# The order of the two products in the wide weight blocks of a two-layer decoder trunk

## The chip, the cores and the metric

The kernel runs on one core of one Trainium2 chip. The metric is the device time of one execution in microseconds (us). The time before is the median of three runs. The profile is one further execution with the hardware profiler on.

## What is computed

A trunk of two pre-norm residual layers on 256 tokens of width 1024, in float32. Layer 0 mixes tokens with a short gated convolution, layer 1 with dilated window attention in three groups of eight heads. After the mixer each layer has a squared-ReLU MLP (1024 to 4096 to 1024) and a gated input embedding.

```python
for i in range(2):
    hn = rmsnorm(h, norm_mix[i])
    mixed = short_conv_mixer(hn, ...) if i == 0 else dilated_attention_mixer(hn, positions, w_qkv, w_o)
    h = h + mixed
    h = h + squared_relu_mlp(rmsnorm(h, norm_mlp[i]), mlp_w_up[i], mlp_w_down[i])
    ple_gate = sigmoid(rmsnorm(h, norm_ple[i]) @ ple_w_gate[i])
    h = h + ple_gate * (p[i] @ ple_w_proj[i])
return rmsnorm(h, norm_final)
```

Nearly all of the work is in dense products of activations with weights: `w_in`, `w_out`, `w_qkv`, `w_o`, `w_up`, `w_down` and the gates.

## The kernel before, in words

**High and low parts.** TensorE multiplies in a reduced float32 format here (`F32R`). To keep the accuracy, every weight and activation is split into a high part (rounded to that format) and a low part (the rest). A product is then three products: low weight by high activation, high weight by low activation, high weight by high activation.

**Weights.** All weights are packed on the host in the order in which they are used, into slabs of up to eight 128x128 tiles (`make_slabs`, L230). `load_to` (L324) loads slabs from HBM. `split_to` (L333) makes the high part `whi` with a ScalarE copy (L340) and the low part `wlo` with a VectorE subtraction (`sub`, L288 and L289). So `wlo` is always later than `whi` of the same slab.

**Blocks.** `make_plan` (L134) writes out the whole order of the work as a list. Each entry is a block (one 128x128 weight tile times the activations) or a step ("do"). The list fixes the order of TensorE's instructions; the other engines' steps are placed among them by a scheduler, and the steps in `URGENT` get a higher priority. `block` (L351) emits the matmuls of one entry, all through the one call at L374. There are three kinds:

- kind "n" (L358): three products of 256 columns, into one half of a PSUM bank.
- kind "w" (L361), the wide blocks: two products. The low weights times the high activations have 256 columns and go to the first half of the bank. The high weights times both parts of the activations have 512 columns and fill the whole bank. `sums` (L389) later adds the halves. Each output column tile of 128 has a bank of its own; tiles come in pairs, `half` 0 and 1, which take turns on every 128 rows `k` of the contraction.
- kind "t" (L367): three products with the weights as the moving operand.

The wide blocks are used for the third input of the convolution (`sc_in`, tile `acc_X`), for the queries and keys of heads 1 to 7 (`qkv`, `acc_qk`), and for both MLPs (`up`, `acc_u`, and `down`, `acc_d`).

**Order within a wide block.** At L364 the tuple `products` lists the low product first and the high one second. L366 turns the tuple round for `half` 1, except for `qkv`. With `half` 0 and 1 alternating, TensorE's order over a pair of blocks is: low, high, high, low. For `qkv` it is: low, high, low, high. The first matmul into a bank has `start` set, whichever it is.

**Around it.** `h_ready` (L417) makes the high part of the next activations on ScalarE (L422) and the low part on VectorE (L423). `mix_out` (L577) and `up_out` (L581) call it or do the same, and `head_start` (L51) orders the first blocks of an MLP, so that the activations made last are used last. The gate of layer 0 (`gate_out`, L599) and the first `qkv` blocks follow the MLP of layer 0.

Of the kernel before, what the change touches and what calls it, by code (L numbers as in the profile page):

```python
# [213 lines left out]
def width(key):  # L214
    return {"v": GROUPS, "gate1": 4, "proj1": 4}.get(key, 1)
# [32 lines left out]
def tile_trunk(ctx: ExitStack, tc: tile.TileContext, plan, slabs, ap, out):  # L248
# [25 lines left out]
    def bank(name):  # L274
        return psum.tile([P, 2, S], F32, tag="ps", name=name)
# [9 lines left out]
    def flat(t):  # L285
        return t.rearrange("p i s -> p (i s)")
# [16 lines left out]
    for op in plan:  # L303
        if op[0] != "do":
            key = ((*op[4], op[5]), 0) if op[0] == "w" else (op[4], op[5] if op[0] == "n" else 0)
# [38 lines left out]
    def weights(item):  # L344
        si, at = place[item]
        split_to(si + min(LOOK, 1 + si // 3))
        hi, lo = parts[si]
        n = width(item[0]) * P
        return hi[:, at : at + n], lo[:, at : at + n]

    def block(kind, key, k, col, name, half, operand, m=0, cuts=1):  # L351
        name = (*name, half) if kind == "w" else name
        if name not in opened:
            acc[name] = bank("acc_" + "_".join(map(str, name)))
        left[name, half if kind == "n" else 0] -= 1
        whi, wlo = weights((key, k, col))
        x = state[operand][k // 2]
        if kind == "n":  # L358
            dst = acc[name][:, half, :]
            products = ((dst, wlo, x[0][:, k % 2, :]), (dst, whi, x[1][:, k % 2, :]), (dst, whi, x[0][:, k % 2, :]))  # L360
        elif kind == "w":  # L361

            dst = acc[name]
            products = ((dst[:, 0, :], wlo, x[0][:, k % 2, :]), (flat(dst), whi, flat(x[2][:, k % 2, :, :])))  # L364

            products = products[::-1] if half and key != "qkv" else products  # L366
        else:  # L367
            n = width(key) * P // cuts
            whi, wlo = (t[:, m * n : (m + 1) * n] for t in (whi, wlo))
            dst = flat(acc[name])[:, :n]  # L370
            xhi, xlo = (t[:, k % 2, half * P : (half + 1) * P] for t in x[:2])
            products = ((dst, xhi, whi), (dst, xhi, wlo), (dst, xlo, whi))
        for n, (to, a, b) in enumerate(products):
            nc.tensor.matmul(  # L374
                to,
                a,
                b,
                start=n == 0 and name not in opened,
                stop=n == len(products) - 1 and left[name, half if kind == "n" else 0] == 0,
                skip_group_check=True,  # L380
            )
            opened.add(name)
# [414 lines left out]
    for op in plan:  # L797
        if op[0] != "do":
            block(*op)
        elif op[1] in URGENT:  # L800
            with tc.high_priority(offset=HURRY):
                steps[op[1]](*op[2:])
        else:
            steps[op[1]](*op[2:])
# [87 lines left out]
```

## Time and profile before

| what | value |
|---|---|
| time, median of 3 runs | 785.04 us (784.73 to 785.06) |
| the profiled execution's own time | 785.37 us |
| its span, first to last instruction | 783.5 us |
| PE (TensorE matmul) busy | 772.6 us, 99% of the span |
| PEld (TensorE weight load) busy | 703.1 us, 90% |
| DVE (VectorE) busy | 575.8 us, 73% |
| ACT (ScalarE) busy | 439.7 us, 56% |
| POOL (GpSimd) busy | 167.6 us, 21% |
| HBM traffic over the span | 179 GB/s |

The profiled execution is 0.33 us over the median of the runs, and 1.9 us of its time lie outside the span. Matmuls are pipelined: the profile draws a matmul's end later than the start of the next, so durations of matmuls overlap, and the time that one costs is read from start to start or from the chain of work that ended last, which counts each stretch once.

### The profile page before, as it was taken

To read this page: it belongs to the slowest core of one execution; us is meant where nothing else is said; L and a number is where in the kernel's file an instruction comes from. 1 tells how busy PE (TensorE), PEld (TensorE's weight loads), DVE (VectorE), ACT (ScalarE), POOL (GpSimd) and SP (SyncE) were. 2 spreads that over 40 slices of the span, in tenths; PEclk is the share of its full clock that TensorE was granted. 3 is DMA by queue.
4 is the path that set the end of the run, shared out by engine and by line. 5 is a ranking of instruction groups with operands and counts; after the bars stand their busy time and mean duration, and the time that the engine had idled before them with its cause. 6 is when DMAs were issued, how large, how long until landed. Compare 5 with 4: busy or idle time off the path is not lost.

```text
span 783.5 us, 12521 instructions
## 1 busy us (share of the span) xinstructions
PE 772.6 (99%) x4858; PEld 703.1 (90%) x4858; DVE 575.8 (73%) x831; ACT 439.7 (56%) x674; POOL 167.6 (21%) x109
## 2 busy tenths in 40 slices
PE   9999999999999999999999999999999999999995
PEld 9999998888888899989989989989988888888884
DVE  6997779898566668888768768767598887655654
ACT  7654565565444446557655655655575555444452
POOL 0000000000000000177867867865000000000001
PEclk9999999999999999999999999999999999999998
DMA  8966555656565554555555455556456565565521
GB/s 288 313 199 191 177 189 177 197 177 202 189 194 187 191 180 147 184 191 156 156 173 163 149 174 163 152 170 194 157 165 187 190 190 191 187 190 194 188 80 54
DMA packets 41819, 140.97 MB, mean 180 GB/s; under 512 B 4768, under 2 KB 5152, under 8 KB 41760
## 3 DMA queue, kind: packets, MB, share of 16 engines
q1 hardware_dynamic: 41328, 139.61, 55.8%
q8 instruction: 38, 0.62, 0.3%
q10 hardware_dynamic: 432, 0.56, 0.2%
q14 instruction: 21, 0.17, 0.1%
HBM read 139.10 MB, written 1.05 MB: 179 GB/s over the span
## 4 chain that ended last, share of the span: by engine, by line
PE 95%; DVE 2%; issue 1%; DMA 1%; ACT 0%; POOL 0%; SPq 0%; POOLq 0%; ACTq 0%
PE acc_u L374 23%; PE acc_d L374 23%; PE acc_qk L374 15%; PE acc_v L374 9%; PE acc_o L374 6%; PE acc_g L374 5%; PE acc_C L374 3%; PE acc_B L374 3%; PE acc_X L374 3%; PE acc_p L374 1%; PE o L693 1%; PE sc L654 1%; PE tp L672 1%; DVE wlo L289 1%; PE sc L651 1%
## 5 line engine op out<-in xcount | busy, mean ns | idle before, releaser
L289 DVE TENSOR_TENSOR wlo<-raw,whi 128x1024 fp32r<-128x1024 f32 (+3 forms) x274 | 350.6, 1285 | 161.9 <-ACT whi L340 159.6
L340 ACT ACTIVATE whi<-raw 128x1024 fp32r<-128x1024 f32 (+3 forms) x274 | 278.0, 1016 | 225.7 <-PE acc_d L374 77.1
L374 PE MATMUL acc_u<-x,whi 128*128 128x512 f32 x512 | 160.9, 396 | 0.0
L374 PE MATMUL acc_d<-u,whi 128*128 128x512 f32 x512 | 160.8, 395 | 0.0
L374 PE MATMUL acc_qk<-x,whi 128*128 128x512 f32 (+1 forms) x432 | 134.8, 369 | 0.8 <-DVE x L423 0.8
L446 POOL TENSOR_TENSOR n<-v,power 128x4 f32<-128x4 f32 (+1 forms) x6 | 5.6, 937 | 521.5 <-DVE v L466 519.4
L374 PEld LDWEIGHTS acc_d<-u,wlo 128*128 128x128 f32 x512 | 96.2, 188 | 22.7
L374 PEld LDWEIGHTS acc_u<-x,wlo 128*128 128x128 f32 x512 | 96.2, 188 | 22.6
L374 PE MATMUL acc_qk<-x,wlo 128*128 128x256 f32 x384 | 107.5, 281 | 0.0
L374 PE MATMUL acc_u<-x,wlo 128*128 128x256 f32 x512 | 101.2, 278 | 0.0
L374 PE MATMUL acc_d<-u,wlo 128*128 128x256 f32 x512 | 100.9, 278 | 0.0
L374 PEld LDWEIGHTS acc_qk<-x,whi 128*128 128x128 f32 x432 | 77.7, 188 | 14.8 <-DVE x L423 1.2
L621 POOL TENSOR_TENSOR rot<-qk,sinr 16x512 f32<-16x512 f32 x44 | 78.3, 1781 | 3.0
L374 PEld LDWEIGHTS acc_u<-x,whi 128*128 128x128 f32 x512 | 77.9, 189 | 0.1
L374 PEld LDWEIGHTS acc_d<-u,whi 128*128 128x128 f32 x512 | 78.0, 189 | 0.0
L374 PEld LDWEIGHTS acc_qk<-x,wlo 128*128 128x128 f32 x384 | 72.3, 189 | 0.2 <-ACT x L422 0.2
L374 PE MATMUL acc_v<-whi,x 128*128 128x384 f32 x256 | 68.8, 339 | 0.0
L618 POOL TENSOR_TENSOR qk<-qk,cosr 128x512 f32<-128x512 f32 x22 | 36.7, 1669 | 52.4 <-DVE qk L394 41.9
L374 PEld LDWEIGHTS acc_v<-whi,x 128*128 128x128 f32 x256 | 46.6, 188 | 0.0
L374 PE MATMUL acc_o<-y,whi 128*128 128x256 f32 x256 | 46.0, 283 | 0.0
L627 POOL TENSOR_TENSOR qk<-qk,rot 48x512 f32<-48x512 f32 x22 | 42.9, 1949 | 1.7
L374 PE MATMUL acc_v<-wlo,x 128*128 128x384 f32 x128 | 42.8, 335 | 0.0
(169 smaller groups left out, 1040.0 us busy)
## 6 DMA issues: line engine op xcount, KB each, us to landing
raw<-in_w SPq DMA_DIRECT2D x231, 512.0 KB, 3.6
raw<-in_w SPq DMA_DIRECT2D x32, 384.0 KB, 3.1
raw<-in_w SPq DMA_DIRECT2D x9, 256.0 KB, 5.2
h<-in_xT SPq DMA_DIRECT2D x4, 256.0 KB, 5.9
out<-ht SPq DMA_DIRECT2D x3, 256.0 KB, 2.0
mask<-in_mask SPq DMA_DIRECT2D x2, 256.0 KB, 4.3
gain<-in_gain SPq DMA_DIRECT2D x2, 256.0 KB, 4.3
pt<-in_pT ACTq DMA_DIRECT2D x1, 256.0 KB, 3.2
```

Of the source, the lines that this page charges most:

```text
L289: nc.vector.tensor_tensor(out, a, f32(b), ALU.subtract)
L340: nc.scalar.activation(hi[:, :width], t[:, :width], AF.Copy)
L374: nc.tensor.matmul(to, a, b, start=n == 0 and name not in opened, stop=n == len(products) - 1 and left[name, half if kind == "n" else 0] == 0,
L446: nc.gpsimd.tensor_tensor(y, v, power[:, : v.shape[1]], ALU.pow)
L618: engine.tensor_tensor(t, p, both(cosr), ALU.mult)
L621: engine.tensor_tensor(r[dst : dst + 16], p[src : src + 16], sinr[src : src + 16].unsqueeze(1).to_broadcast([16, 2, S]), ALU.mult,)
L627: engine.tensor_tensor(t[:48], t[:48], r[:48], ALU.add)
L651: nc.tensor.matmul(ps[:, :S], q[:, 0, own], k[:, 1, :], start=n == 0, stop=n == 2)
L654: nc.tensor.matmul(ps[:, (g + 1) * P : (g + 2) * P], t[:, 0, own], t[:, 1, own], start=True, stop=True)
L672: nc.tensor.transpose(ps[n // 2][:, n % 2, b * P : (b + 1) * P], sm[:, n * P : (n + 1) * P], ident)
L693: nc.tensor.matmul(ps[:, 0, b * P : (b + 1) * P], v12[:, b, g * P : (g + 1) * P], t[:, g, b * P : (b + 1) * P], start=False, stop=g == 1, ...
```

## The change

One line of `block` is changed. The tuple is now turned round for every wide block except those of `qkv`, so the 512-column product with the high weights comes first and the 256-column product with the low weights second, in both halves. `qkv` keeps low first. Over a pair of blocks TensorE's order becomes: high, low, high, low. The blocks, their operands, their banks and the number of instructions stay the same.

```diff
@@ -363,7 +363,7 @@
             dst = acc[name]
             products = ((dst[:, 0, :], wlo, x[0][:, k % 2, :]), (flat(dst), whi, flat(x[2][:, k % 2, :, :])))
 
-            products = products[::-1] if half and key != "qkv" else products
+            products = products if key == "qkv" else products[::-1]
```

## Rows read from the trace of the kernel before

**Rows 1.** The page, busy time by engine, and the chain's shares by engine.

```profile
PE 772.6 (99%) x4858; PEld 703.1 (90%) x4858; DVE 575.8 (73%) x831; ACT 439.7 (56%) x674; POOL 167.6 (21%) x109
...
PE 95%; DVE 2%; issue 1%; DMA 1%; ACT 0%; POOL 0%; SPq 0%; POOLq 0%; ACTq 0%
```

**Rows 2.** The chain in order of time: start, length, work, instructions; pieces of layer 0.

```profile
15.23 1.40 PE acc_X L374 x8
...
35.65 2.10 PE acc_X L374 x12
...
38.30 3.50 PE acc_X L374 x20
...
53.31 5.58 PE acc_X L374 x32
58.88 5.76 PE acc_B L374 x48
...
104.77 22.30 PE acc_u L374 x128
127.30 66.89 PE acc_u L374 x384
194.20 89.17 PE acc_d L374 x512
```

**Rows 3.** The chain again, pieces of layer 1.

```profile
335.22 16.65 PE acc_qk L374 x96
...
400.54 11.11 PE acc_qk L374 x64
...
566.79 22.50 PE acc_u L374 x128
```

**Rows 4.** PE's timeline inside a run of query and key blocks: start, drawn length.

```profile
401.77 0.28 PE L374 MATMUL acc_qk<-x,wlo 128*128 128x256 f32 x1
401.89 0.39 PE L374 MATMUL acc_qk<-x,whi 128*128 128x512 f32 x1
...
411.25 0.40 PE L374 MATMUL acc_qk<-x,whi 128*128 128x512 f32 x1
```

**Rows 5.** PE's timeline at the end, projection products of 512 columns, kind "t".

```profile
766.79 0.39 PE L374 MATMUL acc_p<-whi,p 128*128 128x512 f32 x1
767.02 0.39 PE L374 MATMUL acc_p<-wlo,p 128*128 128x512 f32 x1
767.24 0.62 PE L374 MATMUL acc_p<-whi,p 128*128 128x512 f32 x2
...
768.15 0.39 PE L374 MATMUL acc_g<-whi,x 128*128 128x512 f32 x1
```

**Rows 6.** Stretches: length, busy (instructions) of each engine, PEclk, DMA share, GB/s.

```profile
194.20:283.30 89.10, 89.10 (x513) 77.73 (x513) 51.59 (x60) 40.91 (x51) 0.00 (x0) 1.00 0.58 189
...
335.20:351.80 16.60, 16.60 (x98) 14.51 (x97) 15.03 (x19) 8.42 (x15) 10.94 (x6) 1.00 0.61 189
```

**Rows 7.** Timelines of PE, then DVE, at the head of the MLP of layer 1.

```profile
566.62 0.28 PE L374 MATMUL acc_u<-x,wlo 128*128 128x256 f32 x1
566.84 0.73 PE L374 MATMUL acc_u<-x,whi 128*128 128x512 f32 x2
567.41 0.40 PE L374 MATMUL acc_u<-x,wlo 128*128 128x256 f32 x2
...
566.30 0.89 DVE L423 SCALAR_TENSOR_TENSOR x<-hr,gains,x 128x256 fp32r<-128x256 f32 x2
```

**Rows 8.** The chain once more, between the gate of layer 0 and the attention.

```profile
305.63 0.60 DVE gs L601
306.23 1.13 DVE wlo L289
...
320.68 0.87 DVE wlo L289
322.00 1.46 PE acc_qk L374 x10
```

## The prediction

> **What bounds the kernel now.** I read the page first [rows 1]: TensorE's matmuls are busy 99% of the span, and the chain of work that ended last runs over TensorE for 95% of it. VectorE and ScalarE have a quarter and more of their time free. So a nanosecond saved on TensorE in such a stretch is a nanosecond of the whole, and I need the price of a block, to a tenth of a percent.
>
> That price can't come from the drawn durations, since matmuls overlap (a 512-column matmul is drawn 0.39 us long, and the next starts after 0.23 [rows 4]). It comes from the chain in order of time, where each stretch counts once: length divided by blocks, two instructions to a wide block. The reader is to see two prices for the same two matmuls. Where pairs run low, high, high, low, the down projection takes 89.17 us for 512 instructions, 348.32 ns a block, and the up projection 66.89 us for 384, 348.39 ns [rows 2]. Where every block runs low, high (queries and keys), a run of 96 takes 16.65 us, 346.88 ns a block [rows 3].
>
> The third view is TensorE's own timeline inside such a run, away from its ends. From the high product at 401.89 to the one at 411.25 there are 27 blocks (the rows between repeat the pattern): 9.36 us, 346.67 ns a block [rows 4]. So the steady price of strict alternation is 346.67 ns, and a run's ends add a few hundredths of a microsecond.
>
> Last, the stretches: the granted clock is 1.00 (of 2.4 GHz) in both the down projection and a run of queries and keys, and weight loads are busy 87% of the time in each (77.73 of 89.10 us and 14.51 of 16.60 [rows 6]). Neither clock nor weight traffic sets the two stretches apart.
>
> **Why I put the difference down to the order.** Streams of one size show what each matmul costs without any mixing. The 256-column products of the convolution take 5.76 us for 48, 120.0 ns each [rows 2]. The 512-column products at the end take 766.79 to 768.15, 1.36 us for six, 226.7 ns each [rows 5]. Together 346.7 ns: exactly the alternating price. Alternation therefore costs nothing over its parts, and low, high, high, low costs about 1.65 ns a block more. Two high products in a row and two low ones in a row are what only the dearer pattern has.
>
> **The change part by part.** *What it touches.* Of each pair, only half 0 is turned round; half 1 is high first already. Wide blocks outside `qkv`: 512 of up and 512 of down (two layers of 128 plus 384 plus 512 instructions, over two), and 64 of the convolution's third input. 1088 blocks lie in 544 pairs; nothing is added or removed, no DMA, no instruction of another engine.
>
> *MLPs.* By the chain, layer 0 spends 22.30 + 66.89 + 89.17 = 178.36 us on 512 blocks [rows 2]. At 346.67 ns they take 177.49: 0.87 less. I take 0.85, leaving 0.02 for the ends of the runs (the 96-instruction run costs 16.65 against 48 × 0.34667 = 16.64). Layer 1 repeats it with 22.50 for its first piece [rows 3], whose extra 0.20 is a stall that I treat below. Both layers: -1.70 us. The bounds: by the dearest run of queries and keys, 11.11 us for 32 blocks or 347.19 ns [rows 3], the gain is 178.36 - 177.76 = 0.60 a layer, -1.20 in all; by the steady price and no ends, -1.74. I choose near the second, since these runs are 64 to 256 blocks long and the ends weigh little.
>
> *Convolution input.* Its 64 blocks take four pieces of 1.40 (the first is shown), one of 2.10, one of 3.50 and two of 5.58 (one shown), 22.36 us [rows 2]; at the steady price 22.19, -0.17. The pieces are of four to sixteen blocks, so ends weigh more here: I take -0.10, bounds 0 and -0.17.
>
> *The first block of an MLP.* High first needs the low part of the activations, which low first does not. In layer 0 the pieces before and after meet without a gap. In layer 1 TensorE starts the low product at 566.62 and the high one at 566.84, 0.10 us later than the 0.12 that such a step takes, since VectorE makes the low activations from 566.30, two of them in 0.89 us, the first ready near 566.75 [rows 7]. After the change the high product comes first and still can't start before 566.84; the low product then falls behind it instead of into the wait. Price +0.12 us (one low step); bounds 0 (the next high product, 0.34 us behind, absorbs it) and +0.22 (the whole wait).
>
> *The first use of a slab.* High first asks for `whi` a step earlier and for `wlo` a step later. `whi` is the older of the two, and TensorE has no idle time inside the up and down runs, so I cost it at nothing. The cover is the slabs split ahead; were it gone, the wait would move to the low product and be shorter by the high product's 0.23 us. Half 1 still ends with its low product, so slabs and banks come free in the same order as now.
>
> *Where the saved time goes.* After the MLP of layer 0, the chain passes to VectorE for the gate (305.63 to 322.00), with weight splits of 0.87 to 1.13 us in it [rows 8]. That chain starts from the gate's last products, so it moves forward with them; I cost it at nothing. If the order of VectorE's work changes there, a split more or less in the chain is ±1 us; that is a rival.
>
> *Sum.* -1.70 - 0.10 + 0.12 = -1.68 us. The profiled execution, 785.37, would become 783.69. It stands 0.33 above the median of the runs, so the runs would show 785.04 - 1.68 = 783.36 us, 0.21% less. A measurement of this kernel can tell about 0.2%, 1.57 us, from no change: the forecast lies just beyond that edge, and the chances are split accordingly.
>
> **A rule against it.** The same 768 columns in two matmuls cost 346.67 ns in one order and 348.3 in the other [rows 2, 4]. The Trainium skill, TensorE: Matmul & The Clock Gate, section Back-to-back issue gap, gives the gap of a warm matmul by its column count alone, N / 2.4 + 2.5 ns. By that a block takes 325 ns in any order, and the change brings 0 us. The trace speaks against the figure (both prices are over 20 ns higher) and, less surely, against the independence of order.
>
> **The rivals.** *Order does nothing.* The 1.65 ns could belong to something else that sets up and down apart from queries and keys, such as which tiles are read. For it: no row shows up or down in alternating order. Against: the convolution's input, which reads other tiles, shows 5.58 / 16 = 348.75 with the paired order [rows 2], and the sum of the parts fits alternation. Time: 785.04 us, or 785.16 with the late first block.
>
> *Low after high into the same bank is what costs.* This one ends slower. Queries and keys run low then high into a bank, then go to the other bank; they never write low onto the columns that high has just written. Up and down do it once a pair. If that one step held the whole excess, 2 × 1.65 = 3.3 ns, the change would double it: 350.0 ns a block, +1.65 × 1088 = +1.8 us, 786.8 us. It decides wherever an up block comes out above 348.4 ns. Against it: the 512-column products of the end go high, low, high into one bank at 226.7 ns each, with no excess [rows 5]; but there all three cover the same columns.
>
> *The gate's chain is reshuffled.* A scheduler places VectorE's instructions among each other, and a changed TensorE order may move a weight split into or out of the 16 us in which VectorE sets the pace [rows 8]. One split is 0.87 to 1.13 us, say 1.0: 782.4 us if one leaves, 784.4 if one enters. For it: splits stand in that chain more than once. Against: both orders take the same operands and almost the same time, so the scheduler has little to react to.
>
> **How the numbers follow.** The forecast, alternation at about 346.7 ns, has 0.67; within it the edge at 783.47 is 0.11 us away, and the bounds reach from 783.1 (-1.74 - 0.17 + 0) to 784.1 (-1.20 - 0 + 0.22), so I give it 0.44 faster and 0.23 same. Order does nothing: 0.13, same. Low after high: 0.07, slower (its 786.8 lies just beyond the edge at 786.61). A split leaves: 0.07, faster; one enters: 0.06, same. Faster 0.51, same 0.42, slower 0.07. The likeliest gives 783.36 us. The range from 782.5 to 784.9 holds the forecast and its bounds, nearly all of the late split and the fast half of the split that leaves: 0.67 + 0.06 + 0.04, and with a little of the case without effect about 0.8.
>
> **What would show it.** In the profile after, the chain's piece of the down projection should be 88.75 us instead of 89.17, and the long piece of up 66.56 instead of 66.89, on TensorE's timeline with single rows high, low, high, low and no x2. The piece of the convolution should fall from 5.58 to about 5.55, the queries and keys should stay. The first piece of up in layer 1 should be 22.4, with the wait on the low activations ahead of a high product. Any of these stretches above its old length would put the bank rival ahead; unchanged lengths, the first one. If the stretches shrink as said and the time does not, the saved time went into the chain from 305 to 322 us, which would then be longer than 16.4 us by what is missing.

## The result, and the profile after

The changed kernel takes 787.58 us (median of 8 runs, 786.9 to 790.55) against 785.28 us of the kernel before (8 runs, 784.73 to 785.78). The ratio is 1.0038, with a 95% interval of 1.0026 to 1.0049: slower by 0.38%, where 0.21% faster was forecast. The profiled execution took 787.52 us, 2.15 us more than that of before.

The chain of waits in order of time (start, length, work, instructions), changed kernel; the pieces that answer to [rows 2, 3] and [rows 8]:

```profile
15.02 1.41 PE acc_X L374 x8
...
35.49 2.13 PE acc_X L374 x12
...
38.08 3.47 PE acc_X L374 x20
...
53.05 5.65 PE acc_X L374 x32
...
104.67 22.62 PE acc_u L374 x128
...
127.52 67.84 PE acc_u L374 x384
195.36 90.45 PE acc_d L374 x512
...
324.39 1.45 PE acc_qk L374 x10
...
337.61 16.65 PE acc_qk L374 x96
...
569.31 22.85 PE acc_u L374 x128
...
592.40 66.56 PE acc_u L374 x384
658.97 88.75 PE acc_d L374 x512
```

The reader is to see one program at two prices. In layer 1 the long piece of up and the piece of down have exactly the forecast lengths, 66.56 and 88.75 us, 346.67 ns a block. In layer 0 the same two pieces, with the same order and the same shapes, take 67.84 and 90.45 us: 353.3 ns a block, dearer than the 348.3 of before [rows 2]. The convolution shows both within one pair of columns: 2.13 us for 6 blocks is 355, 3.47 for 10 is 347. Queries and keys, which the change leaves alone, are unchanged at 16.65.

The balance closes. Layer 0: 180.91 against 178.36, +2.55. Layer 1: 178.16 against 178.56, -0.40. The convolution (four pieces of 1.41, then 2.13, 3.47, 5.65 and one of 5.64): 22.53 against 22.36, +0.17. Together +2.32; the start-up before the first convolution block was 0.21 us shorter. The sum is 2.11 of the 2.15 us.

Stretches of the changed kernel, TensorE alone (length, busy with instructions, granted clock, DMA share, GB/s), layer 0 and layer 1:

```profile
127.52:195.30 67.78, 67.78 (x386) 1.00 0.59 187
592.40:658.90 66.50, 66.50 (x386) 1.00 0.62 190
```

The granted clock is 1.00 in both, so the clock is not the difference. TensorE's own timeline, first in layer 0, then in layer 1, shows what is:

```profile
139.73 0.40 PE L374 MATMUL acc_u<-x,whi 128*128 128x512 f32 x1
139.97 0.28 PE L374 MATMUL acc_u<-x,wlo 128*128 128x256 f32 x1
140.08 0.40 PE L374 MATMUL acc_u<-x,whi 128*128 128x512 f32 x1
140.31 0.28 PE L374 MATMUL acc_u<-x,wlo 128*128 128x256 f32 x1
140.43 0.40 PE L374 MATMUL acc_u<-x,whi 128*128 128x512 f32 x1
140.67 0.28 PE L374 MATMUL acc_u<-x,wlo 128*128 128x256 f32 x1
140.79 0.40 PE L374 MATMUL acc_u<-x,whi 128*128 128x512 f32 x1
...
619.63 0.39 PE L374 MATMUL acc_u<-x,whi 128*128 128x512 f32 x1
619.86 0.28 PE L374 MATMUL acc_u<-x,wlo 128*128 128x256 f32 x1
...
620.67 0.39 PE L374 MATMUL acc_u<-x,whi 128*128 128x512 f32 x1
```

No wait stands in either. Three blocks take 1.06 us from 139.73 to 140.79, and 1.04 from 619.63 to 620.67; in the first the steps go round in a pattern that repeats every three blocks (high products of 0.24, 0.23 and 0.24). In the nanoseconds of the trace its blocks take 350, 350 and 360, again and again, those of layer 1 346 or 347. So strict alternation has two steady patterns, 346.7 and 353.3 ns a block, and here it stays in the one it is in: down of each layer goes on in the pattern that up left. Below they are called the cheap and the dear pattern.

### The profile page after: what moved, and what is told of

It reads as the page before. It is cut to its first block, busy times and chain, and to the rows that moved or that the text cites. A ratio compares the mean times of both kernels' runs of the same rounds, so it can differ in the third digit from the quotient of the medians.

```text
span 785.7 us, 12525 instructions
## 1 busy us (share of the span) xinstructions
PE 774.0 (99%) x4858; PEld 704.7 (90%) x4858; DVE 575.6 (73%) x831; ACT 439.5 (56%) x674; POOL 167.6 (21%) x109
## 4 chain that ended last, share of the span: by engine, by line
PE 95%; DVE 2%; issue 1%; DMA 1%; ACT 0%; POOL 0%; POOLq 0%; SPq 0%; ACTq 0%
PE acc_u L374 23%; PE acc_d L374 23%; PE acc_qk L374 15%; PE acc_v L374 8%; PE acc_o L374 6%; PE acc_g L374 5%; PE acc_C L374 3%; PE acc_B L374 3%; PE acc_X L374 3%; PE acc_p L374 1%; PE o L693 1%; PE sc L654 1%; PE tp L672 1%; DVE wlo L289 1%; PE sc L651 1%
## 5 line engine op out<-in xcount | busy, mean ns | idle before, releaser
L374 PE MATMUL acc_u<-x,whi 128*128 128x512 f32 x512 | 179.9, 396 | 0.1
L374 PE MATMUL acc_d<-u,whi 128*128 128x512 f32 x512 | 179.3, 395 | 0.0
L374 PE MATMUL acc_u<-x,wlo 128*128 128x256 f32 x512 | 143.6, 281 | 0.0
L374 PE MATMUL acc_d<-u,wlo 128*128 128x256 f32 x512 | 143.6, 280 | 0.0
L374 PEld LDWEIGHTS acc_u<-x,whi 128*128 128x128 f32 x512 | 96.0, 188 | 23.1 <-PE acc_o L374 0.3
L374 PEld LDWEIGHTS acc_d<-u,whi 128*128 128x128 f32 x512 | 96.0, 187 | 22.5
```

Of the source, the lines that this page charges most:

```text
L374: nc.tensor.matmul(to, a, b, start=n == 0 and name not in opened, stop=n == len(products) - 1 and left[name, half if kind == "n" else 0] == 0,
```

## The experiments: what decides between the two patterns

Each kernel below is the changed kernel with the edit shown; times of before are from the same chip and series.

### Low first everywhere

```diff
-            products = products if key == "qkv" else products[::-1]
```

> Every wide block runs low first, as queries and keys do. Bank theory (a low product onto columns that the high product has just written lets TensorE settle into 353.3 ns a block; a low product into another bank does not): no such step is left, so all up, down and convolution runs at 346.7 ns, down 88.75 us in both layers, time 783.5 us. Entry theory (any strict alternation can run at 346.7 or 353.3 ns, and the first product of the run decides, high first being the risky one): the same 783.5. Chance theory (every break before a run draws one of the two patterns anew, whatever the order): some runs at 353.3, time between 784 and 790 us, differing between executions by 0.5 to 3.4 us.

790.06 us (789.94 to 790.24, 4 runs), ratio to before 1.0068 [1.0053, 1.0083]. Chain, this kernel:

```profile
127.55 67.84 PE acc_u L373 x384
195.40 90.45 PE acc_d L373 x512
...
337.67 16.65 PE acc_qk L373 x96
...
592.16 67.84 PE acc_u L373 x384
660.01 90.45 PE acc_d L373 x512
```

This was the test that I had thought safe in either theory, and it failed both. Up and down now run exactly as queries and keys do, low then high, and take the dear pattern in both layers, while queries and keys keep the cheap one. Neither the bank nor which product comes first can be the reason.

### The low product into another bank, and a low start with the banks as changed

Both kernels hold back the second product of half 0 until half 1 is out, which gives high 0, low 1, high 1, low 0, and low 0, high 1, low 1, high 0. The edit of the first is shown, without its changes to `start` and `stop`; the second has `and half` in place of `and not half`.

```diff
-            products = products if key == "qkv" else products[::-1]
+            products = products[::-1] if key != "qkv" and not half else products
...
+        if kind == "w" and key != "qkv":
+            if half:
+                todo.append(held_back.pop())
+            else:
+                held_back.append(todo.pop())
```

> Order over a pair: high 0, low 1, high 1, low 0. TensorE sees high, low, high, low and a run starts with high, as after the change, but every low product goes to another bank than the high one before it. Bank theory: no run at 353.3 ns, 783.5 us. Entry theory: the first runs of both layers at 353.3 ns as after the change, about 787.5 us. Chance theory: a mixture, 784 to 790 us.

> Order over a pair: low 0, high 1, low 1, high 0. A run starts with low, and every low product but the first goes onto columns that the high product has just written, as after the change. Bank theory: runs at 353.3 ns, 786 to 790 us. Entry theory: all runs at 346.7 ns, 783.5 us. Chance theory: a mixture, 784 to 790 us.

The first took 787.77 us (787.19 to 790.34), ratio 1.0050 [1.0031, 1.0069]: layer 0 dear (down 90.45), layer 1 cheap (88.75), although no low product follows a high one into the same bank any more. The second took 790.44 us (790.35 to 792.35), ratio 1.0079 [1.0064, 1.0094], dear in both layers although each run starts low. The chain of the first, both layers:

```profile
195.44 90.45 PE acc_d L382 x512
...
658.68 88.75 PE acc_d L382 x512
```

Bank theory and the theory of the first product are out. The chance theory does not fit layer 0 either: its up and down ran dear in the profiles of the changed kernel and of these three, and the four runs of the first of the three lie within 0.3 us of each other.

### Queries and keys high first too

```diff
-            products = products if key == "qkv" else products[::-1]
+            products = products[::-1]
```

> As after the change, and queries and keys high first too. There are 336 wide blocks of queries and keys in 22 stretches that other work breaks up. Bank theory and entry theory: some or all of these stretches rise from 346.7 to 353.3 ns a block, up to 336 x 6.65 = +2.2 us over the changed kernel, so 787.5 to 790 us. If queries and keys stay at 346.7 ns, something else in their tiles or surroundings protects them, and both theories lack a part.

Queries and keys stay cheap: 16.64 us for the 48 blocks of head 1, 11.10 or 11.11 for each run of 32. Both theories lacked a part, as the last sentence had it. The time is 790.26 us (787.36 to 790.48); the profiled execution, 787.36, has layer 0 dear and layer 1 cheap, and the three runs above 790 have no trace. At the head of layer 1's MLP, where up starts behind a wait of 0.3 us, chance stays possible: its first piece took 22.85 us in the changed kernel's profile and 22.43 in this one, with the same code.

What remains is what runs on TensorE just before: 256-column products ahead of up in layer 0 (`acc_o`), of the convolution's pieces (`acc_B` and `acc_C`) and, two of them, of up's second piece (the norm's sums at L479). Ahead of queries and keys stand the 384-column products of the values, in seven of the thirteen stretches that the chain shows. The other six, of 32 blocks each, stand right behind the scores, products of 256 and 128 columns; one of them in the changed kernel's chain:

```profile
402.48 0.44 PE sc L654 x4
402.93 11.11 PE acc_qk L374 x64
```

They are cheap as well. So narrow products ahead do not always make a run dear, and the stream theory below has to be read with that exception.

### Wide products ahead of the MLP, and narrow ones as a control

A step ahead of `head_start` issues products that nobody reads, two of 512 columns in one kernel, four of 256 in the other, and two of 384 in a third.

```diff
-    plan = head_start(up, "u", x, ("up_out",))
+    plan = [("do", "lead", x, 512, 2)] + head_start(up, "u", x, ("up_out",))
...
+        for n in range(count):
+            nc.tensor.matmul(ps[:, :cols], ones_r, x[:, :cols], start=True, stop=True)
```

> The changed kernel with two extra products of 512 columns (a constant by the first activations, never read) ahead of each MLP. Stream theory (strict alternation keeps whichever of its two patterns it starts in; a stream of 256-column products ahead of it starts the slow one, wider products or a wait start the fast one): up and down of both layers at 346.7 ns a block, up's first piece in layer 0 about 22.2 us, down 88.75 us twice, time about 784.3 us, of which 0.9 us are the extra products. Tile theory (something in the tiles or surroundings of up and down of layer 0 is slow): layer 0 stays at 353.3, down 90.45, time 788 to 791 us.

> The control to the run before: four extra products of 256 columns in the same place, nearly the same extra time (4 x 120 ns against 2 x 227). Stream theory: layer 0 stays at 353.3 ns a block (down 90.45 us), time 788 to 791.5 us. If a mere break or any extra product were enough to start the fast pattern, this would be at 784.3 too.

> As the run with two extra products of 512 columns ahead of each MLP, but of 384 columns, the width of the value products that stand ahead of queries and keys. Stream theory: all of up and down at 346.7 ns, about 784.7 us. If 384 columns do not set the fast pattern, layer 0 stays at 353.3 and the time is 787.5 to 791 us, and queries and keys must owe their fast pattern to something else.

Chains of the kernel with 512 columns, then of the control:

```profile
104.94 0.47 PE lead L388 x2
105.41 22.19 PE acc_u L374 x128
127.60 0.23 PE ssq L485 x2
127.83 66.56 PE acc_u L374 x384
194.39 88.75 PE acc_d L374 x512
...
566.67 0.70 PE lead L388 x2
567.37 22.19 PE acc_u L374 x128
...
589.79 66.56 PE acc_u L374 x384
656.35 88.75 PE acc_d L374 x512
```

```profile
104.78 0.47 PE lead L388 x4
105.25 22.61 PE acc_u L374 x128
...
128.09 67.84 PE acc_u L374 x384
195.93 90.45 PE acc_d L374 x512
```

The same 0.47 us of extra work in layer 0 changes everything behind it when it is two wide products, and nothing when it is four narrow ones. With 512 columns all of up and down is cheap in both layers and the time is 784.74 us (10 runs, 784.43 to 785.16; ratio 0.9993 [0.9984, 1.0002]), 2.8 us under the 787.58 of the changed kernel, which was measured in another series, although work was added. The control takes 790.98 us (789.91 to 792.38), ratio 1.0074, and is dear in both layers. With 384 columns, the width of the values, the profiled execution is cheap throughout too (up 66.56, down 88.75 in both layers), at a median of 784.65 us; two of its ten runs stand at 788.1 and 788.2 and have no trace, so this start may be less sure.

### Queries and keys behind narrow products

The first kernel puts eight of the unread 256-column products ahead of a stretch of queries and keys in each of heads 1 to 7. The second makes group 0 of head 1 a stream of 48 real 256-column products, between the values and the other 32 wide blocks.

```diff
-            ("w" if h else "n", "qkv", k, (i, g, h), ("qk", h, g), i, "x3") for k in ks for i in (0, 1)
+            ("w" if h and (g or h > 1) else "n", "qkv", k, (i, g, h), ("qk", h, g), i, "x3") for k in ks for i in (0, 1)
```

> The changed kernel with eight extra products of 256 columns ahead of the first query and key stretch of each of heads 1 to 7, 7 x 8 x 120 ns = 6.7 us of extra work. Stream theory: these stretches (16 blocks each, and what follows them without a break) rise from 346.9 to about 353 ns a block, the first, of head 1, with all its 48 blocks from 16.65 to about 16.95 us. Tile theory: they stay at 346.9.

> The changed kernel, but group 0 of head 1's queries and keys in blocks of three 256-column products, so a stream of 48 products of the kind that stands ahead of up now stands between the values and the other 32 wide blocks of head 1. Stream theory in its strict form (such a stream starts the slow pattern): these 32 blocks take 11.3 us instead of 11.1. In its weak form (such a stream keeps the pattern that was there, and the values set the fast one): they stay at 11.1 us. Tile theory: 11.1 us too; the later heads stay as they are in every case.

The eight left queries and keys cheap: 16.64 us for the 48 blocks behind them, where the stream theory had 16.95. The one run took 797.39 us; against the changed kernel's profile that is 6.6 us of added products (7 × 0.94) and 3.0 us of layer 1, whose up and down ran dear too (67.84 and 90.45). The eight are products of one constant that stays the same, and ran at 0.94 us, 117.5 ns each, faster than the 120.0 of a real stream [rows 2]. The real stream made the run dear. It differs from the eight in number as well, 48 against 8, so which of the two matters is not shown. TensorE's timeline of the second kernel at the seam, and its chain:

```profile
343.42 0.40 PE L374 MATMUL acc_qk<-x,whi 128*128 128x256 f32 x2
343.66 0.28 PE L374 MATMUL acc_qk<-x,wlo 128*128 128x256 f32 x1
343.78 0.40 PE L374 MATMUL acc_qk<-x,whi 128*128 128x512 f32 x1
```

```profile
338.08 17.06 PE acc_qk L374 x112
```

48 products at 120 ns are 5.76 us; the 32 wide blocks are left with 11.30, 353 ns each, where they took 11.1 before. The very tiles and order that are cheap in every other profile are dear behind a stream of 256-column products, in the one execution that was taken. That speaks against the tiles, and for the strict form of the stream theory with this stream; the scores' narrow products do not have that effect.

### A lead pair out of the work itself

The first pair of blocks of a wide run goes high, high, low, low, then strict alternation. The main part of the edit:

```diff
...
+        if kind != "w" or key == "qkv":
+            run["new"] = True
+        elif half:
+            if held_back:
+                todo.insert(1, held_back.pop())
+        elif run.pop("new", False):
+            held_back.append(todo.pop())
...
```

> The changed kernel, but the first pair of blocks of each wide run goes high, high, low, low, so two 512-column products of the work itself stand ahead of the alternation, at no cost. Stream theory: if two wide products are enough and the two low ones behind them don't undo it, up and down at 346.7 ns in both layers and 783.4 us, faster than both kernels. If the two low products in a row bring the slow pattern back, layer 0 at 353.3 ns and 787 to 790.5 us.

> The run before with a lead pair (high, high, low, low) kept, and one more wherever the small products of the norms break a wide run (two 256-column products inside up, four or two inside the others). Stream theory: the second piece of up and down then keep 346.7 ns a block in both layers, up 66.56 and down 88.75 us, 783.4 us, faster than both kernels. If a lead pair does not outlast the whole of up and down, or the low pair behind it undoes it, up's second piece is at 353.3 and the time at 787 to 790 us.

> A lead pair at the first row k of every output column pair as well as at the run's start, so once in every 16 blocks of up and every 64 of down, without one behind the norm's products. Stream theory: each lead pair sets the fast pattern anew and costs the 3.3 ns that a pair of the kernel before costs; up at about 346.9 ns a block but for the one column behind the norm's products, down 346.7 to 346.8, 783.5 us. Chance theory (each break draws anew): a mixture of columns at 346.7 and 353.3, 785 to 789 us.

With the pair at the start of runs alone, up's first pieces become cheap (22.19 and 22.43 us) and the convolution too; but behind the two 256-column sums of the norm (L479 of the changed kernel) the second piece is dear again, 67.84 us, and down follows with 90.45: 789.28 us (788.94 to 790.08), ratio 1.0050. In layer 0 of this kernel:

```profile
105.07 22.19 PE acc_u L384 x128
127.26 0.23 PE ssq L489 x2
127.49 67.84 PE acc_u L384 x384
```

In the kernel with 512 columns the same two sums follow a first piece of the same length (22.19 us) and, but for its first pair, of the same order, and the second piece stayed at 66.56. So the sums do not decide by themselves, and a cheap run can differ from another in something that its length does not show; what that is stays open.

The second kernel sets `run["new"]` at the norms' small products as well, so that a lead pair follows them. Its chain:

```profile
126.74 66.56 PE acc_u L384 x384
193.30 88.75 PE acc_d L384 x512
...
565.61 22.84 PE acc_u L384 x128
588.70 66.57 PE acc_u L384 x384
655.27 88.75 PE acc_d L384 x512
```

It takes 783.35 us (11 runs, 782.83 to 784.28) against 785.05, ratio 0.9978 [0.9969, 0.9987]: 0.22% faster than the kernel before, and faster than the changed one. Only up's first piece in layer 1, which starts behind a wait, and one of the convolution's pieces (3.53 us for 10 blocks) stayed dear, although a lead pair stands at the head of each.

A lead pair is no cure in itself. The third kernel has `or k == 0` behind `run.pop("new", False)`. Placed so once in every column, inside a run that is already cheap, it made the run dear: 67.67 us for up's second piece and 90.43 for down, 789.73 us, ratio 1.0057 [1.0043, 1.0071]. In TensorE's timeline of that kernel the first column behind the norm's sums, right after a lead pair (every column starts at `k` 0, so one stands there too, other than expected), runs at 346.9 ns; from the next lead pair on the columns run at 353.

## Why the prediction was wrong

**What bounds the kernel** held: every gain or loss in a block's price on TensorE came out in the time. VectorE's chain between gate and attention moved as a whole (its first `acc_qk` at 324.39 instead of 322.00 [rows 8], while down ended about 2.4 us later), so that rival was not met.

**The step that failed** is the term for the MLPs, -1.70 us: it took the steady price of queries and keys [rows 4] for the price of the order. It is the price of that order in one of two patterns, and rows of before held only that one. It measured -0.40 in layer 1, of which the two long pieces gave the full -0.75, and +2.55 in layer 0. The bounds of the step, 346.67 to 347.19 ns, were drawn from queries and keys alone, so they left the dear pattern out; the range built on them missed the result.

**The supporting argument** was a coincidence in part. That 120.0 and 226.7 add up to 346.7 looked like proof that alternation costs nothing over its parts. The same parts also run at 353.3.

**The rival that the order does nothing** named the right weakness, something that sets up and down apart from queries and keys, but as tiles; what was shown to matter is what TensorE ran just before. **The bank rival** gave nearly the measured time, 786.8, and for the wrong reason: low products sent to other banks ran just as dear. The Trainium skill, TensorE: Matmul & The Clock Gate, section Back-to-back issue gap, gives its formula by the column count for an isolated matmul, and says that in a stream weight loads and matmuls set the spacing together; the prediction left that out. This trace, with 346.7 and 353.3 ns for the same instructions, agrees with no price by column count alone. The loads are drawn alike in both patterns, 187 to 189 ns, so their length does not tell the two apart.

**The convolution** was put at -0.10 and came to +0.17, by the same cause. **The first block of up in layer 1** was put at +0.12. Its piece as a whole ran dear (22.85 us), but the timeline shows the block: it ends 0.97 us after the start of the last two products of `acc_o` (568.77 to 569.74), against about 0.80 before (566.38 to 567.41, less the second high product of 0.23), so 0.17 later and inside the bounds 0 and 0.22. That upper bound was called the whole wait, but holds the low step of 0.12 as well; the wait was 0.10. **Slabs and banks** cost nothing, as said: no wait appeared in the long runs.

**The spread of the runs** fits as well. Six of the eight runs lie between 786.9 and 788.0, two at 790.2 and 790.6. The step of about 3 us is that of 448 blocks of layer 1 in the dear pattern, 448 × 6.65 = 3.0 us; the kernel with low first everywhere, whose profile shows them dear, took 790.24. Those two runs have no trace, so for them it is an inference.

The order of before (low, high, high, low) came out at 348.3 to 348.4 ns in all long pieces of its one profile: it pays 1.65 ns a block more than the cheap pattern and shows no dear one there. Of its 49 runs on record 46 lie between 784.1 and 785.8 us; three stand at 786.1, 786.8 and 787.0, without a trace.

## What to carry to other kernels

A price read from one stretch holds for another only if what comes before it is the same, too: look for a second stretch with the same instructions and another neighbour before building a sum on it. A regular stream of matmuls can have more than one steady pattern; print the steps from start to start, and compare several runs of the same code within one trace. An order that comes out the same in every stretch can be worth more than one that is faster at its best.

## What was not expected of the hardware

Two patterns of one instruction stream at granted clock 1.00, 346.7 and 353.3 ns for 768 columns, kept over up to 448 blocks (155 us) without a wait. Two products of 512 columns ahead of a run, 0.47 us, moved it from one to the other; the two of 256 columns inside up could move it either way (from dear to cheap in layer 1 of the changed kernel, from cheap to dear in the kernel with a lead pair) or leave it (cheap with two products of 512 columns ahead). Forty-eight products of 256 columns in a stream made queries and keys dear, the scores' 256 and 128 columns left them cheap. What TensorE carries from one product to the next is open: no run here shows it.
